# Low halves of the top-k's weights on VectorE, softmax 16 ticks earlier, two splits of v moved

## The chip, the cores and the metric

The kernel runs on one core of one Trainium2 chip. The metric is the device time of one execution in microseconds (us). The kernel before took 2052.27 us as the median of three runs (2051.45, 2052.27 and 2065.59). Engines are named as the profile names them: PE is TensorE's matmul part and PEld its weight load, DVE is VectorE, ACT is ScalarE, POOL is GpSimd, and SP is SyncE, which issues the weight transfers.

## The reference

The program computes a three-block network on 256 tokens of width 1024, in f32: a first block with attention, a recurrent unit and a memory attention, then a PEER expert layer, then two layers of four mixers and a feed-forward each. The change lies in the expert layer alone:

```
q = (h @ w_q), 8 heads x 2 halves x 128
sc = q . sub_keys                      # 8 x 2 x 128 scores a token
top_v, top_i = top_k(sc, 16)           # per half
cand = top_v[0] + top_v[1]             # all pairs of the two halves
best, pos = top_k(cand, 16); idx = the pair's expert number (of 16384)
gate = softmax(best)
act = gelu(u[idx] . h)
out = sum over heads and k of (gate * act) * v[idx]
```

The kernel does not gather rows of u and v. It multiplies with all 16384 rows, as 128 blocks of 128 experts, and zeroes what no token chose: a matrix of gates, built from one-hot rows, multiplies the acts.

## The kernel before, in words

**Weights.** All weights come as one stream of 128x128 blocks in f32. Eight blocks are a slot. SP loads two slots with one transfer (`raw`, two buffers). For each slot ACT writes the rounded high half `whi` (L93) and a second engine writes the low half `wlo` = raw - whi (L96); there are three buffers of each. The second engine is DVE, or POOL where `pool_share` says so: (1, 1) is set in the top-k after the projection of a head pair is traced, and (0, 1) after the top-k. Each weight block then costs three matmuls of 256 columns (L178 to L180: high by high, high by low, low by high), so a slot is 24 matmuls. The transfer for a `raw` buffer waits until both low halves of the pair that was in it have been written.

**Order.** The instructions of each engine stand in one fixed order, which a planner makes when the kernel is built. It plans with its own costs: of what is ready it takes the earliest traced first, and the splits of a slot have priority over the rest. At run time each engine works through its order strictly and waits where an operand is late. `issue_after(x)` puts an instruction behind x on x's engine.

**Ticks.** Side work is traced by generators (`add`, `tick`, `_step`), stepped each time two weight blocks have been used: a tick is two weight blocks, or six matmuls. The PE instructions of a step go behind the last matmul traced.

**The expert layer** (`peer`, L744) has these stages.

1. Top-k (`topk`, L954). Eight units (four head pairs by two token halves), 22 ticks apart (`TK_PACE`). A unit makes scores on PE (`sc`, L970) and then works on DVE alone: `top16` for four score rows, the candidate sums `cd` (L985), `top16` for two heads, index arithmetic (`tf` L977, `ij`, `ijf` L996 to L1005), two one-hot picks (`oh` L1008 and L1011, `sl` L1013). `TK_LAST` ticks after the last unit the softmax `gates` is traced (`ge` L1020, Exp on ACT at L1022, then L1023 to L1025 into `slg`); 6 ticks later `turn` transposes `sl1`, `sl2` and `slg` on PE (`ptk`, L248). Meanwhile PE runs the rest of the query projection and then blocks of u (`u_block`, L766: eight weight blocks, `pu`, then a gelu into `ha` or `hb` at L773). The number of u blocks done when the top-k ends is `early`.
2. First build (`build`, L792, with c0 = 0). 32 steps of eight tokens: DVE makes one-hots (`e` L810 and L812, `e1g` L815), PE multiplies them (`pgb`, L823), ACT copies (`gs` L827), DVE adds (L830) and multiplies the gates into the acts of the blocks 0 to 63 (L836), or only stores gates where an act does not exist yet (L841). Beside it run 64 further u blocks (`u_while`). The acts of the blocks `early` to 63 come in this stage and are kept apart.
3. The first of v. `weighted(b, g)` splits the gated act of block b into `ga`, a high half on ACT (L191) and a low half on DVE (L192). `collapse` (L868) multiplies the kept acts, four blocks at a time, with their gates. Three u blocks (`FILL`) are traced with the collapses.
4. The v loop. For b from 0 to 124: trace `weighted(b + 2)`, then eight weight blocks of v into `acc`; after each odd b one further u block until all 128 are done. The second build (`more`, c0 = 64) runs beside it, one step in 10 ticks. `weighted(64)` needs it complete, so what is left of it then is traced at once (`finish`, L877).

Of the kernel before, what the change touches and what calls it, by code (L numbers as in the profile page):

```python
# [7 lines left out]
F32 = mybir.dt.float32  # L8
# [5 lines left out]
ALU = mybir.AluOpType  # L14
# [14 lines left out]
N_HA = 96  # L29
HALF = 64  # L30
TK_PACE = 22
TK_LAST = 64
FILL = 3
T_OH = 8
PACE = {0: 7.5, HALF: 10}
# [22 lines left out]
class Stream:  # L58
# [3 lines left out]
    def __init__(self, K, pool, w):  # L62
        self.K, self.pool, self.w = K, pool, w
        self.order = []
        self.ticked = 0
        self.raw = None
        self.cur = None
        self.pool_share = (0, 1)

    def _dram(self, i):  # L70
        return self.w[i].rearrange("p (b c) -> p b c", c=P)
# [7 lines left out]
    def _slot(self):  # L79
        K, nc = self.K, self.K.nc  # L80
        n = len(self.order) // 8
        with K.tc.high_priority(offset=PRIO):
            if n % 2 == 0 and n:
                self.raw = self.pool.tile([P, 16, P], F32, tag="raw", name="raw", bufs=RAW_BUFS)
                m = min(16, N_BLOCKS - n * 8)
                step = 16 if n > 2 else 8
                for b in range(0, m, step):
                    e = min(b + step, m)
                    nc.sync.dma_start(out=self.raw[:, b:e, :], in_=self._dram(n // 2)[:, b:e, :])
            src = self.raw[:, (n % 2) * 8:(n % 2) * 8 + 8, :]  # L90
            hi = self.pool.tile([P, 8, P], F32R, tag="whi", name="whi", bufs=SLOT_BUFS)
            lo = self.pool.tile([P, 8, P], F32R, tag="wlo", name="wlo", bufs=SLOT_BUFS)
            self.on_scalar = nc.scalar.activation(out=hi, in_=src, func=AF.Copy).ins  # L93
            m, d = self.pool_share
            eng = nc.gpsimd if n * m % d < m and n else nc.vector
            i = eng.tensor_tensor(out=lo, in0=src, in1=hi.bitcast(F32), op=ALU.subtract)  # L96
            if eng is nc.vector:
                self.on_vector = i.ins
            else:
                self.on_pool = i.ins  # L100
        self.cur = (hi, lo)

    def blks(self, w, k, c, n=1):
# [25 lines left out]
def blocks(*tiles):  # L129
    return [t[:, i, :] for t in tiles for i in range(t.shape[1])]  # L130


class Core:
# [614 lines left out]
    def peer(self):  # L748
# [4 lines left out]
        tc, nc, a, ws = self.tc, self.nc, self.a, self.ws  # L753
        with ExitStack() as st:
# [6 lines left out]
            ga = [p.tile([P, 2, S], F32R, tag=f"ga{i}", name="ga") for i in range(2)]  # L761
# [3 lines left out]
            def h(b):  # L765
                return ha[:, b, :] if b < N_HA else hb[:, b - N_HA, :]  # L766
# [8 lines left out]
            def u_while(task, most, early):  # L775

                nonlocal ahead
                while task in self.tasks and ahead < most:
                    u_block(ahead, h(ahead + HALF if early <= ahead < HALF else ahead))
                    ahead += 1  # L780
                self.finish(task)
            ahead = 0
            with tc.tile_pool(name="tk", bufs=2) as tp:
                u_while(self.topk(tp, i1, i2, gt, iot), HALF, HALF)
            with tc.tile_pool(name="peg", bufs=1) as gp:
                hb = gp.tile([P, NBLK - N_HA, S], F32, tag="hb", name="hb")
                ga.append(gp.tile([P, 2, S], F32R, tag="ga2", name="ga"))
                ws.pool_share = (0, 1)
                n2, n1 = T_OH * P, T_OH * HALF
                e = self.tp.tile([P, 2, n2 + n1], F16, tag="ld", name="e", bufs=1)  # L790
                e2s = [e[:, i, 0:n2].rearrange("p (q c r) -> p q c r", c=P, r=2) for i in range(2)]
# [63 lines left out]

                early = ahead
                u_while(self.add(build(0, early), unit=1), HALF + early, early)
                assert ahead >= HALF

                def collapse(b0):  # L860

# [9 lines left out]
                def weighted(b, g):  # L871

                    if b == HALF:
                        self.finish(more)
                    src = h(b)
                    if b >= done:
                        with tc.issue_after(ws.on_vector):  # L877
                            nc.vector.tensor_tensor(out=src, in0=src, in1=h(b - done), op=ALU.mult)
                    self.split(g[:, 0, :], g[:, 1, :], src)
                    return g  # L880


                done = NBLK
                ready = [weighted(0, ga[0])]
                late = list(range(early, HALF, 4))
                for i in range(FILL):
                    for b in late[i * len(late) // FILL:(i + 1) * len(late) // FILL]:
# [11 lines left out]
                    self.mm3(acc[c // 2][:, c % 2, :], wh, wl, g[:, 0, :], g[:, 1, :],  # L899
                             first and c % 2 == 0, last and c % 2 == 1)  # L900

                ready.append(weighted(1, ga[1]))
                for b in range(NBLK - LAST):
                    if b + 2 < NBLK - LAST:
                        ready.append(weighted(b + 2, ga[(b + 2) % 3]))
# [9 lines left out]
            with tc.tile_pool(name="per", bufs=1) as gp:  # L915
# [6 lines left out]
                for c in range(KD):  # L922
                    for i, g in enumerate(tail):
                        v_cols(c, NBLK - LAST + i, g, False, i == LAST - 1)
                    if c % 2:
                        for d in (c - 1, c):
                            xc = self.x[:, d, :]
                            nc.vector.scalar_tensor_tensor(out=xc, in0=acc[d // 2][:, d % 2, :], scalar=1.0 / G_SCALE,
                                                           in1=xc, op0=ALU.mult, op1=ALU.add)
# [26 lines left out]
    def topk(self, tp, i1, i2, gt, iot):  # L956
        nc, a, ws = self.nc, self.a, self.ws
# [57 lines left out]
        def gates(t):  # L1015

            bv = bvs[t].rearrange("p (h k) -> p h k", k=16)
            e = tp.tile([P, 8, 16], F32, tag="ge", name="ge")
            sm = tp.tile([P, 2, 8], F32, tag="gs", name="gs")
            nc.vector.tensor_tensor(out=e, in0=bv, in1=bv[:, :, 0:1].to_broadcast([P, 8, 16]), op=ALU.subtract)  # L1020
            with self.tc.issue_after(ws.on_scalar):
                nc.scalar.activation(out=e, in_=e, func=AF.Exp)  # L1022
            nc.vector.tensor_reduce(out=sm[:, 0, :], in_=e, axis=AX.X, op=ALU.add)  # L1023
            nc.vector.reciprocal(out=sm[:, 1, :], in_=sm[:, 0, :])
            nc.vector.scalar_tensor_tensor(out=slg[t].rearrange("p (h k) -> p h k", k=16), in0=e, scalar=G_SCALE,  # L1025
                                           in1=sm[:, 1, :, None].to_broadcast([P, 8, 16]),
                                           op0=ALU.mult, op1=ALU.mult)

        def turn(t):

            ts = slice(t * P, t * P + P)
            pt = self.bg.tile([P, 3, P], F32, tag="bg", name="ptk")
            for i, sl in enumerate((sl1[t], sl2[t], slg[t])):
                self.transpose(pt[:, i, :], sl)
            nc.scalar.activation(out=i1[:, ts], in_=pt[:, 0, :], func=AF.Copy)
            nc.scalar.activation(out=i2[:, ts], in_=pt[:, 1, :], func=AF.Copy)
            nc.scalar.activation(out=gt[:, 0, ts], in_=pt[:, 2, :], func=AF.Copy)
            nc.vector.tensor_tensor(out=gt[:, 1, ts], in0=pt[:, 2, :], in1=gt[:, 0, ts], op=ALU.subtract)
            if t == 0:
                self.dump("sl1", sl1[0])  # L1040
                self.dump("sl2", sl2[0])
                self.dump("slg", slg[0])
# [3 lines left out]
        def picks():  # L1046
            with self.tc.issue_after(ws.on_vector):
                nc.gpsimd.tensor_copy(io, self.cst[:, None, C_IO:C_IO + 16].to_broadcast([P, 32, 16]))
            for hq in range(4):
                for t in range(2):  # L1050
                    while hq not in qts:
                        yield 1
                    unit(hq, t, qts[hq])
                    if hq == t == 1:
                        with self.tc.issue_after(ws.on_pool):
                            nc.gpsimd.tensor_copy(iot, self.cst[:, C_IO:C_IO + P, None].to_broadcast([P, P, 2]))
                    yield TK_PACE

            yield TK_LAST
            for t in range(2):  # L1060
                gates(t)
            yield 6
            for t in range(2):
                turn(t)
            yield 4

        task = self.add(picks(), unit=1)
        n = self.ld.shape[1] - 4
        for hq in range(1, 4):
            qt = tp.tile([P, 4, S], F32, tag="qt", name="qt")  # L1070
            c0 = 4 * hq + (n if hq == 1 else 0)

            def ev(c, ps):
                nc.scalar.activation(out=qt[:, c - 4 * hq:c - 4 * hq + 2, :], in_=ps, func=AF.Copy)
            self.proj_b(("w_peer_q", 0, 0), 4 * hq + 4, KD, self.hh, self.hl, ev, c0=c0,
                        lead=4 * hq + 4 - c0 if hq == 1 else 0)
            ws.pool_share = (1, 1)
            qts[hq] = Cat(blocks(self.ld[:, 4:4 + n, :], qt[:, n:, :])) if hq == 1 else qt
        return task

# [569 lines left out]
```

## Time and profile before

| what | value |
|---|---|
| median of three runs | 2052.27 us |
| the profiled execution's own time | 2051.29 us |
| its span, first to last instruction | 2049.5 us |
| PE busy, granted clock | 2006.7 us (98%), 0.993 of full |
| DVE busy | 1673.3 us (82%) |
| ACT busy | 1159.0 us (57%) |
| POOL busy | 277.9 us (14%), 146.2 us of it `wlo` |
| transfers | 364.73 MB read from memory, 179 GB/s over the span |

PE's busy share says how much of the span holds matmuls; what is left is idle time. A granted clock of 1.00 is 2.4 GHz, one of 0.50 is 1.2 GHz. POOL is busy with `wlo` from 311 us to 483 us, in the top-k. The top-k's last transposes stand at 485 us, the first product of the first build at 495 us, the first of v at 690 us and the end of the second build at 919 us.

### The profile page before, as it was taken

To read this page: it belongs to the slowest core of one execution; us is meant where nothing else is said; L and a number is where in the kernel's file an instruction comes from. 1 tells how busy PE (TensorE), PEld (TensorE's weight loads), DVE (VectorE), ACT (ScalarE), POOL (GpSimd) and SP (SyncE) were. 2 spreads that over 40 slices of the span, in tenths; PEclk is the share of its full clock that TensorE was granted. 3 is DMA by queue.
4 is the path that set the end of the run, shared out by engine and by line. 5 is a ranking of instruction groups with operands and counts; after the bars stand their busy time and mean duration, and the time that the engine had idled before them with its cause. 6 is when DMAs were issued, how large, how long until landed. Compare 5 with 4: busy or idle time off the path is not lost.

```text
span 2049.5 us, 41488 instructions
## 1 busy us (share of the span) xinstructions
PE 2006.7 (98%) x16818; PEld 1952.2 (95%) x16818; DVE 1673.3 (82%) x3281; ACT 1159.0 (57%) x1906; POOL 277.9 (14%) x173
## 2 busy tenths in 40 slices
PE   8999999999999999989999999999999999999999
PEld 7989999999999999989999889999999989999997
DVE  7877779999999999995568999978555999977554
ACT  6688654445555555544456565566445665466443
POOL 2212207883000000000000101200000101200000
PEclk9999999999999999999999999999999999999999
DMA  5345554454454455454554644555555644554554
GB/s 216 144 133 172 205 205 182 174 197 165 167 183 166 168 184 184 167 184 162 189 195 163 220 162 146 195 195 186 197 194 188 224 158 149 188 188 178 198 195 154
DMA packets 57019, 370.01 MB, mean 181 GB/s; under 512 B 6587, under 2 KB 10236, under 8 KB 13564
## 3 DMA queue, kind: packets, MB, share of 16 engines
q1 hardware_dynamic: 50256, 357.06, 48.4%
q10 hardware_dynamic: 6572, 10.31, 1.7%
q8 instruction: 131, 2.15, 0.4%
q14 instruction: 60, 0.49, 0.1%
HBM read 364.73 MB, written 2.62 MB: 179 GB/s over the span
## 4 chain that ended last, share of the span: by engine, by line
PE 68%; DVE 19%; issue 2%; ACT 2%; DMA 1%; ACTq 0%; DVEq 0%
PE acc L178 5%; PE acc L179 5%; PE acc L180 5%; PE mm L178 5%; PE mm L179 5%; PE mm L180 5%; PE pu L180 3%; PE pu L178 3%; PE pu L179 3%; PE pg L180 3%; PE pg L178 3%; PE pg L179 3%; DVE wlo L96 3%; PE pp L180 2%; PE pp L179 2%
## 5 line engine op out<-in xcount | busy, mean ns | idle before, releaser
L93 ACT ACTIVATE whi<-raw 128x1024 fp32r<-128x1024 f32 x677 | 717.5, 1061 | 738.7 <-DMA raw<-in_w 166.1
L96 DVE TENSOR_TENSOR wlo<-raw,whi 128x1024 fp32r<-128x1024 f32 x618 | 765.6, 1240 | 308.7 <-ACT whi L93 306.5
L180 PE MATMUL pu<-hh,wlo 128*128 128x256 f32 x1024 | 286.5, 280 | 2.1 <-POOL wlo L96 2.1
L178 PE MATMUL pu<-hh,whi 128*128 128x256 f32 x1024 | 285.2, 278 | 1.1 <-ACT whi L93 1.1
L180 PE MATMUL mm<-hh,wlo 128*128 128x256 f32 x1008 | 280.7, 279 | 5.1 <-DVE wlo L96 5.0
L179 PE MATMUL pu<-hl,whi 128*128 128x256 f32 x1024 | 283.8, 277 | 0.0
L178 PE MATMUL mm<-hh,whi 128*128 128x256 f32 x1008 | 281.0, 279 | 0.0
L179 PE MATMUL mm<-hl,whi 128*128 128x256 f32 x1008 | 280.4, 278 | 0.0
L178 PE MATMUL acc<-ga,whi 128*128 128x256 f32 x1000 | 277.4, 280 | 2.3 <-ACT ga L191 2.3
L179 PE MATMUL acc<-ga,whi 128*128 128x256 f32 x1000 | 277.5, 278 | 1.1 <-DVE ga L192 1.1
L180 PE MATMUL acc<-ga,wlo 128*128 128x256 f32 x1000 | 276.6, 278 | 0.0
L180 PEld LDWEIGHTS mm<-hh,wlo 128*128 128x128 f32 x1008 | 190.2, 189 | 8.1 <-DVE wlo L96 6.9
L178 PE MATMUL pg<-hh,whi 128*128 128x256 f32 x704 | 197.3, 280 | 0.0
L180 PE MATMUL pg<-hh,wlo 128*128 128x256 f32 x704 | 196.6, 279 | 0.5 <-DVE wlo L96 0.5
L179 PE MATMUL pg<-hl,whi 128*128 128x256 f32 x704 | 196.4, 279 | 0.0
L180 PEld LDWEIGHTS pu<-hh,wlo 128*128 128x128 f32 x1024 | 193.1, 189 | 2.3 <-POOL wlo L96 2.3
L178 PEld LDWEIGHTS pu<-hh,whi 128*128 128x128 f32 x1024 | 193.3, 189 | 1.7 <-ACT whi L93 1.5
L179 PEld LDWEIGHTS pu<-hl,whi 128*128 128x128 f32 x1024 | 193.1, 189 | 0.0
L178 PEld LDWEIGHTS mm<-hh,whi 128*128 128x128 f32 x1008 | 190.3, 189 | 1.4 <-issue 0.7
L179 PEld LDWEIGHTS acc<-ga,whi 128*128 128x128 f32 x1000 | 189.8, 190 | 1.3 <-DVE ga L192 1.3
L179 PEld LDWEIGHTS mm<-hl,whi 128*128 128x128 f32 x1008 | 190.0, 189 | 1.1 <-issue 0.8
L178 PEld LDWEIGHTS acc<-ga,whi 128*128 128x128 f32 x1000 | 188.1, 189 | 2.6 <-ACT ga L191 2.6
(413 smaller groups left out, 4901.3 us busy)
## 6 DMA issues: line engine op xcount, KB each, us to landing
raw<-in_w SPq DMA_DIRECT2D x336, 1024.0 KB
raw<-in_w SPq DMA_DIRECT2D x5, 512.0 KB
bias<-bias_scr ACTq DMA_DIRECT2D x4, 512.0 KB
bias_scr<-sbb ACTq DMA_DIRECT2D x16, 96.0 KB
cl<-in_cstl ACTq DMA_DIRECT2D x2, 576.0 KB
x<-in_xT SPq DMA_DIRECT2D x4, 256.0 KB
memt<-in_memT ACTq DMA_DIRECT2D x1, 1024.0 KB
keys<-in_keysT ACTq DMA_DIRECT2D x1, 1024.0 KB
```

What stands on the lines that cost most here:

```text
L93: self.on_scalar = nc.scalar.activation(out=hi, in_=src, func=AF.Copy).ins
L96: i = eng.tensor_tensor(out=lo, in0=src, in1=hi.bitcast(F32), op=ALU.subtract)
L178: mm(out, lhsT=wh, rhs=xh, start=start, stop=False)
L179: mm(out, lhsT=wh, rhs=xl, start=False, stop=False)
L180: self.on_pe = mm(out, lhsT=wl, rhs=xh, start=False, stop=stop).ins
```

## The change

All low halves of weights are made on DVE; `pool_share` is gone, and with it the 59 low halves on POOL. `TK_LAST` is 48 ticks in place of 64. In the third stage the splits for v's blocks 0 and 1 are both traced ahead of the collapses and of the three `FILL` blocks; before, that of block 1 was traced behind them. The index pattern `iot` (a POOL copy) names a DVE instruction in its `issue_after`, which orders nothing on POOL.

```diff
-TK_LAST = 64
+TK_LAST = 48
...
-        self.pool_share = (0, 1)
...
-            m, d = self.pool_share
-            eng = nc.gpsimd if n * m % d < m and n else nc.vector
-            i = eng.tensor_tensor(out=lo, in0=src, in1=hi.bitcast(F32), op=ALU.subtract)
-            if eng is nc.vector:
-                self.on_vector = i.ins
-            else:
-                self.on_pool = i.ins
+            i = nc.vector.tensor_tensor(out=lo, in0=src, in1=hi.bitcast(F32), op=ALU.subtract)
+            self.on_vector = i.ins
...
-                ws.pool_share = (0, 1)
...
-                assert ahead >= HALF
+                assert early >= 2 and ahead >= HALF
...
-                ready = [weighted(0, ga[0])]
+                ready = [weighted(b, ga[b]) for b in range(2)]
                 late = list(range(early, HALF, 4))
                 for i in range(FILL):
                     for b in late[i * len(late) // FILL:(i + 1) * len(late) // FILL]:
                         collapse(b)
                     u_block(ahead, h(ahead))
                     ahead += 1
...
-                ready.append(weighted(1, ga[1]))
                 for b in range(NBLK - LAST):
...
-                        with self.tc.issue_after(ws.on_pool):
+                        with self.tc.issue_after(ws.on_vector):
                             nc.gpsimd.tensor_copy(iot, ...)
...
-            ws.pool_share = (1, 1)
```

## Rows read from the trace of the kernel before

**Rows 1.** Windows, the top-k: stretch, us, then each engine's busy us, clock.

```profile
306.00:475.00 169.00, 169.00 (x1482) 168.83 (x1482) 167.25 (x506) 83.08 (x118) 139.85 (x58) 1.00 0.50 181
```

**Rows 2.** Source L970, the scores: count, ns min/median/max, first and last start.

```profile
L970 PE MATMUL sc<-keys,qt x48: 270/275/275, 335.8 to 416.4; 128*128 128x128 f32 x48
```

**Rows 3.** DVE by line, 306:485 us: busy us, mean ns of one, idle before.

```profile
L1008 DVE TENSOR_TENSOR oh<-ijf,io 128x512 f16<-128x512 f16 x16 | 25.1, 1569 | 0.0
L1011 DVE TENSOR_TENSOR oh<-oh,tf 128x512 f16<-128x512 f16 x16 | 23.8, 1485 | 0.3
L985 DVE TENSOR_TENSOR cd<-tv 128x96 f32<-128x96 f32 (+1 forms) x16 | 18.1, 1133 | 0.0
L1003 DVE SCALAR_TENSOR_TENSOR ijf<-ijf 128x32 f16<-128x32 f16 x8 | 14.7, 1838 | 0.0
...
L977 DVE CAST tf<-ti 128x64 f16<-128x64 uint32 x8 | 8.1, 1011 | 0.0
...
L1005 DVE TENSOR_TENSOR ijf<-bi,ijf 128x32 f16<-128x32 uint32 x8 | 8.0, 1001 | 0.0
...
L1001 DVE TENSOR_SCALAR ijf<-ijf 128x32 f16<-128x32 f16 x8 | 5.7, 714 | 0.3
```

**Rows 4.** DVE in order of time: start us, us; POOL idle, then busy.

```profile
469.37 0.27 DVE L985 TENSOR_TENSOR cd<-tv 128x128 f32<-128x128 f32 x1
...
474.84 0.68 DVE L1008 TENSOR_TENSOR oh<-ijf,io 128x512 f16<-128x512 f16 x1
...
475.44 0.18 DVE L1003 SCALAR_TENSOR_TENSOR ijf<-ijf 128x32 f16<-128x32 f16 x1
...
475.56 0.42 DVE L1011 TENSOR_TENSOR oh<-oh,tf 128x512 f16<-128x512 f16 x1
...
475.90 2.34 DVE L1005 TENSOR_TENSOR ijf<-bi,ijf 128x32 f16<-128x32 uint32 x1
```

**Rows 5.** POOL in order of time, its last three low halves.

```profile
475.68 7.82 POOL L96 TENSOR_TENSOR wlo<-raw,whi 128x1024 fp32r<-128x1024 f32 x3 [3.79 <-ACT whi L93]
```

**Rows 6.** POOL by line, whole span.

```profile
L96 POOL TENSOR_TENSOR wlo<-raw,whi 128x1024 fp32r<-128x1024 f32 x59 | 146.2, 2487 | 28.5 <-ACT whi L93 28.3
```

**Rows 7.** PE in order of time at the top-k's end; idle before, releaser.

```profile
478.24 0.38 PE L180 MATMUL pu<-hh,wlo 128*128 128x256 f32 x1 [2.08 <-POOL wlo L96]
...
485.34 0.33 PE L248 MATMUL ptk<-cst,slg 128*128 128x128 f32 x1 [1.13 <-DVE slg L1025]
```

**Rows 8.** Source L830, adds of the two builds, with their shapes.

```profile
L830 DVE TENSOR_TENSOR gs<-gs,pgb x128: 353/368/410, 498.7 to 919.9; 128x204 f32<-128x204 f32 x64, 128x216 f32<-128x216 f32 x64
```

**Rows 9.** DVE in order of time, before the first of v.

```profile
687.53 3.83 DVE L868 TENSOR_TENSOR ha<-ha,hb 128x1024 f32<-128x1024 f32 x4
691.27 1.22 DVE L96 TENSOR_TENSOR wlo<-raw,whi 128x1024 fp32r<-128x1024 f32 x1
692.40 1.09 DVE L192 TENSOR_TENSOR ga<-ha,ga 128x256 fp32r<-128x256 f32 x3
```

**Rows 10.** Windows: before the first of v; two stretches of low clock.

```profile
686.00:700.00 14.00, 12.22 (x91) 11.82 (x90) 11.42 (x17) 5.59 (x11) 0.00 (x0) 0.88 0.51 193
...
693.90:697.50 3.60, 3.60 (x20) 3.60 (x19) 2.29 (x3) 0.68 (x2) 0.00 (x0) 0.53 0.83 296
...
919.00:926.20 7.20, 4.89 (x25) 4.62 (x24) 3.04 (x11) 1.80 (x5) 0.00 (x0) 0.50 0.00 0
```

**Rows 11.** PE in order of time, end of the second build.

```profile
906.31 0.63 PE L823 MATMUL pgb<-e1g,e 128*128 128x128 f16 x8
...
911.28 0.63 PE L823 MATMUL pgb<-e1g,e 128*128 128x128 f16 x8
...
915.38 0.64 PE L823 MATMUL pgb<-e1g,e 128*128 128x128 f16 x8 [3.46 <-DVE e L810]
...
918.35 1.03 PE L823 MATMUL pgb<-e1g,e 128*128 128x128 f16 x8 [2.34 <-DVE e L810]
...
921.69 1.22 PE L178 MATMUL acc<-ga,whi 128*128 128x256 f32 x4 [2.31 <-ACT ga L191]
```

## Prediction

> **What bounds the kernel now.** The page's busy shares come first: PE holds matmuls for 2006.7 of 2049.5 us. The change adds no matmul and takes none away, so it can only move PE's idle time, some 43 us over the whole program, and the stretches in which PE had the lower clock. The windows by stage come next. In the top-k PE is busy without a gap while DVE is at 167.25 of 169 us and POOL at 139.85 [rows 1]: DVE is as full as PE, but nothing on PE waits for it there. What PE does lose near the change lies in three places, read from PE's order of time and its waits.
>
> *End of the top-k*: PE waits 2.08 us for a low half on POOL, then 1.13 us for `slg` [rows 7]. *Before the first of v*: 1.78 us idle of 14, then 3.6 us at about half clock [rows 10]. *End of the second build*: 3.46, 2.34 and 2.31 us, together 8.11 [rows 11], and from 919 us on the clock is at 0.50, which is 1.2 GHz; PE was busy 4.89 us there [rows 10], work of some 2.4 us at full clock, so 2.4 us lost. All three together are worth about 17 us, 0.8% of the time.
>
> **The change, part by part.** The sum is made against the profiled execution's 2051.29 us; the median of the runs is 0.98 us above that, which I add at the end.
>
> *59 low halves leave POOL.* A low half took 2.49 us there [rows 6] and takes 1.22 us on DVE, with a next instruction 1.13 us after its start [rows 9]. While POOL works, some DVE instructions of the top-k last about as long as a POOL one: `ijf` at L1005 took 2.34 us right after POOL began at 475.68 [rows 4, 5]; just before, with POOL idle, the one-hots took 0.68 and 0.42 and `ijf` 0.18, and `cd` 0.27 as POOL was only starting [rows 4]. Against these the means of the stretch [rows 3] give what the overlap costs: L1008 16 x (1.57 - 0.68) = 14.2, L1011 16 x (1.49 - 0.42) = 17.0, L985 16 x (1.13 - 0.27) = 13.8, L1003 8 x (1.84 - 0.18) = 13.3, and with the same 0.18 for L977, L1005 and L1001 6.6, 6.6 and 4.3: 75.8 us of DVE's time, which goes.
>
> The Trainium skill (Perfetto Trace Analysis, Optimizing Scalar/DVE Operations) advises, where DVE is saturated, to move work off it, to ScalarE or even GpSimd, though it adds that for GpSimd this may not help because the two share a port. By the advice alone the change goes the wrong way and the sum would be that of the last rival below; rows 3 to 5 bear out the caveat.
>
> *They come to DVE.* PE uses a slot (24 matmuls) in 24 x 169/1482 = 2.74 us [rows 1]. The top-k now ends 32 weight blocks sooner, that is 10.9 us, four slots, so 55 of the 59 lie in it: 55 x 1.13 = 62.2 us. DVE's work up to the softmax falls by 75.8 - 62.2 = 13.6 us. It stays full: over 306 to 475 us, 167.25 less 75.8 x 169/179 leaves 95.7, plus 62 slots x 1.13 = 70, 166 of 169.
>
> The new wait is that each low half now stands in DVE's strict order behind top-k work. Behind it are the matmuls of its slot and, through the release of `raw`, SP's next transfer. What hides it: POOL's 2.49 us hid completely in this stretch (PE full [rows 1]), so DVE may be at least 2.49 - 1.22 = 1.3 us late free of cost. No row shows DVE doing top-k and low halves together for long. From below: no wait at all. From above: units follow each other every (416.4 - 335.8 - 0.8)/5 = 16.0 us on PE [rows 2]; a unit has 95.7/8 = 12.0 us of DVE work, and 16.0 us hold 5.8 slots, 6.6 us; if the planner took a unit for short and put it all ahead, 2.6 us a unit, 21 us for eight. The second build is the nearest case, DVE full with low halves in its order and no wait in PE until its end. I take +2.
>
> *End of the top-k.* The low half that PE waited 2.08 us for comes 2.49 - 1.22 = 1.3 us sooner: -1.3. The Exps and what ACT does around them stay. The transposes: PE gets there 10.9 + 1.3 us sooner, at 472.0 in the old count, and `slg`, old 485.3, comes 13.6 sooner, at 471.7. That is even, with nothing to spare: I leave the old 1.13 as it is. Ends: -1.1, and +4 if all 59 low halves still come ahead.
>
> *Fewer u blocks in the top-k.* Sixteen ticks are 32 weight blocks, four u blocks. The first build adds 204 elements = 4 tokens x 51 blocks [rows 8], so `early` was 51 and becomes 47. The 64 blocks beside the first build and the three of `FILL` stay, so u blocks left for the v loop go from 10 (128 - 118; 216/4 = 54 = 118 - 64 [rows 8]) to 14. They move four blocks of PE work from the top-k to the v loop at no cost on PE. DVE multiplies four more late gates at the v loop's end, when the second build is long over: hidden; if DVE were still full there, four short multiplications of 256 elements.
>
> *Collapses.* Thirteen late blocks took 691.27 - 687.53 = 3.74 us on DVE, straight ahead of a low half and of the splits of `ga` [rows 9]. They become 17: +1.15 us. Block 0's split, traced ahead of the collapses already, still ran after all of them, in one row of three with its successors' [rows 9]; so I expect little from tracing block 1's early too. Its bounds: -3.5 (idle and low clock gone) to 0. I take 0, and +1.15 for the collapses, as PE waits for what they hold up. `iot` without its order has only constants to wait for, and nobody waits for it but SP's queue: 0.
>
> *End of the second build.* Its step k falls due at tick 11 + 10k of the v loop. `weighted(64)` forces the rest when 62 blocks of v and 10 of u are through, 72 x 4 = 288 ticks: steps 28 to 31 are forced, the four rows of products [rows 11]. With 14 blocks of u it is 304 ticks: step 29 is due at 301, so two are forced. From step 29 to block 64 of v DVE's chain took 921.69 - 911.28 = 10.4 us [rows 11]. PE now has 3 ticks, then blocks 62 and 63, 11 ticks x 0.685 = 7.5 us, and the products' own 1.9. That leaves 1 us of wait; as DVE must also make the low halves and splits of these blocks I take 3. So -5.1 of 8.11; the low clock I leave. Ends: 0 and -10.5.
>
> Sum: +2 - 1.3 + 1.15 - 5.1 = -3.2; 2051.29 - 3.2 + 0.98 = 2049.0 us.
>
> **The rivals.**
> 1. *DVE's order holds up PE* (slower). The price per unit is up to 2.6 us. It decides where waits in the top-k pass 5 us. For it: 98% load, no comparable row, and collapses that ran 3.7 us ahead of a low half that PE then waited for [rows 9]. Against it: splits have priority, and the second build. Halfway (10 us, 8 more than I took) it gives 2057, in full 2068; low clock behind each wait could add more. Chance 0.22.
> 2. *The second build's end keeps its wait*, DVE being full up to it whatever is forced: 2049.0 + 5.1 = 2054. The spacing of 4.1 and 3.0 us between forced steps speaks for DVE as the limit; 10.9 us more for the same steps speaks against. Chance 0.13.
> 3. *All of it goes well*: no waits in the top-k (-2), `slg` on time (-1.1), the first of v without a wait (-4.6), the build's end without wait or low clock (-5.4): 2036. Chance 0.11.
> 4. *The long DVE rows are not POOL's doing.* Then nothing is freed and 62 us come on top of a DVE with 2 us to spare: some 2051 + 60 = 2111. Rows 4 and 5 speak plainly against it. The advice of the Trainium skill's page named above would lead here. Chance 0.02.
>
> **How the numbers follow.** My own case has 0.52, with 2042 to 2054 as its range (build's end -10.5 to 0, top-k 0 to 5). The range reaches to 2060, over most of rival 1's halfway case and rival 2, and down to 2039, into rival 3; what is left out is about 0.15. Within 1% of 2052.27, about what a measurement of this kernel can tell from no change, is 2031.7 to 2072.8. All three idle places gone would be 17 us, not 20.5: faster 0.02. Slower needs rival 1 in full with low clock, or rival 4: 0.05. The rest, 0.93, is within.
>
> **What would show it.** POOL free of `wlo`; L1008, L1011, L1003, L985 near 0.68, 0.42, 0.18 and 0.27 us; adds of 188 and 200 elements in place of 204 and 216; two products in a row at the second build's end with under 4 us of idle PE; the transposes some 11 us sooner. PE waits on `wlo` of DVE above 5 us in the top-k would make the prediction wrong, and so would three waits still standing before block 64 of v.

## The result: a half per cent faster, and what the profile after shows

Over 20 runs each, the changed kernel took 2049.92 us in the median (2037.88 to 2056.41) and the kernel before 2059.74 us (2050.50 to 2073.20). The ratio is 0.9949 with a 95% interval of [0.993, 0.9967]: 10.5 us faster, between 6.8 and 14.4. The profiled execution took 2048.76 us, 2047.0 of it span, at a mean granted clock of 0.997.

The time forecast (2049.0 us) and its case (within 1%) hold. The size of the change does not: I had summed -3.2 us, and measured is three times that. The time still came out because the three runs shown of before were low ones: two of the three are the second and third lowest of its twenty, and their median is 7.5 us under the median of all.

The page after says PE 2010.7 us busy (98%), DVE 1656.2 (81%), POOL 132.0 (6%); POOL has no `wlo` any more. The lines of DVE in the top-k (busy us, mean ns of one, idle before) answer to [rows 3]:

```profile
L93 DVE TENSOR_TENSOR wlo<-raw,whi 128x1024 fp32r<-128x1024 f32 x57 | 69.1, 1214 | 6.3 <-ACT whi L92 3.5 <-PE pu L173 2.6
L1000 DVE TENSOR_TENSOR oh<-ijf,io 128x512 f16<-128x512 f16 x16 | 10.9, 682 | 0.0
...
L1003 DVE TENSOR_TENSOR oh<-oh,tf 128x512 f16<-128x512 f16 x16 | 6.7, 419 | 0.0
...
L977 DVE TENSOR_TENSOR cd<-tv 128x96 f32<-128x96 f32 (+1 forms) x16 | 4.1, 257 | 0.0
...
L969 DVE CAST tf<-ti 128x64 f16<-128x64 uint32 x8 | 1.5, 186 | 0.0
L997 DVE TENSOR_TENSOR ijf<-bi,ijf 128x32 f16<-128x32 uint32 x8 | 1.4, 181 | 0.0
...
L995 DVE SCALAR_TENSOR_TENSOR ijf<-ijf 128x32 f16<-128x32 f16 x8 | 1.4, 177 | 0.0
```

Each fell to the value that the few undisturbed rows of before had shown: 1569 to 682 ns, 1485 to 419, 1133 to 257, 1838 to 177. The windows (stretch, its length, then PE, PEld, DVE, ACT and POOL with counts, clock) say what that bought:

```profile
306.00:464.00 158.00, 157.96 (x1384) 157.85 (x1385) 151.68 (x567) 77.35 (x110) 1.00 (x1) 1.00 0.50 181
917.00:920.50 3.50, 3.50 (x18) 3.50 (x18) 0.17 (x1) 0.00 (x0) 0.00 (x0) 0.50 0.30 124
1000.00:1025.00 25.00, 25.00 (x215) 25.00 (x214) 13.60 (x18) 12.29 (x18) 0.00 (x0) 1.00 0.53 186
```

With all low halves on it DVE has 6 us of 158 to spare, where before it had under 2 of 169 [rows 1], and PE loses nothing there. The other two stretches come up below. PE in order of time, first at the top-k's end, answers to [rows 7]:

```profile
464.85 0.39 PE L172 MATMUL pu<-hh,whi 128*128 128x256 f32 x1 [0.37 <-ACT whi L92]
465.07 0.28 PE L173 MATMUL pu<-hl,whi 128*128 128x256 f32 x1
466.11 0.39 PE L174 MATMUL pu<-hh,wlo 128*128 128x256 f32 x1 [0.76 <-DVE wlo L93]
...
470.65 0.27 PE L242 MATMUL ptk<-cst,slg 128*128 128x128 f32 x1
```

The transposes wait for nothing. What is late instead is the slot behind the softmax. ACT and DVE, each in order of time, show why:

```profile
460.23 0.31 ACT L1014 ACTIVATE ge<-ge 128x128 f32<-128x128 f32 x1
460.56 1.28 ACT L767 ACT_TABLE_LOAD   x1
461.85 0.39 ACT L767 ACTIVATE ha<-pu 128x256 f32<-128x256 f32 x1
462.24 1.28 ACT L1014 ACT_TABLE_LOAD   x1
463.54 0.31 ACT L1014 ACTIVATE ge<-ge 128x128 f32<-128x128 f32 x1
463.76 1.04 ACT L92 ACTIVATE whi<-raw 128x1024 fp32r<-128x1024 f32 x1
```

```profile
463.88 0.29 DVE L1015 TENSOR_REDUCE gs<-ge 128x8 f32<-128x128 f32 x1 [3.02 <-ACT ge L1014]
...
464.83 1.23 DVE L93 TENSOR_TENSOR wlo<-raw,whi 128x1024 fp32r<-128x1024 f32 x1
```

A gelu between the two Exps makes ACT load its tables twice more; the high half stands behind all of it, and DVE, waiting 3.02 us for the second Exp, has the low half behind the rest of the softmax. ACT's order there was the same before the change, and PE waited for its high half then too, 0.47 us that my prediction left out:

```profile
475.66 0.39 PE L178 MATMUL pu<-hh,whi 128*128 128x256 f32 x1 [0.47 <-ACT whi L93]
```

Before the first of v, DVE's order answers to [rows 9], and PE's waits lie under it:

```profile
675.99 4.64 DVE L861 TENSOR_TENSOR ha<-ha,hb 128x1024 f32<-128x1024 f32 x4
680.53 1.23 DVE L93 TENSOR_TENSOR wlo<-raw,whi 128x1024 fp32r<-128x1024 f32 x1
681.67 0.43 DVE L861 TENSOR_TENSOR ha<-ha,hb 128x256 f32<-128x256 f32 x1
682.00 1.10 DVE L186 TENSOR_TENSOR ga<-ha,ga 128x256 fp32r<-128x256 f32 x3
```

```profile
680.31 0.39 PE L172 MATMUL pu<-hh,whi 128*128 128x256 f32 x1 [0.64 <-ACT whi L92]
...
682.49 0.39 PE L173 MATMUL acc<-ga,whi 128*128 128x256 f32 x1 [1.67 <-DVE ga L186]
```

The splits of both blocks, now traced ahead of all collapses, still run behind them: 2.31 us idle where it was 1.78. The end of the second build (PE in order of time) answers to [rows 11], and the source view of the adds to [rows 8]:

```profile
908.66 0.63 PE L816 MATMUL pgb<-e1g,e 128*128 128x128 f16 x8
...
911.90 0.63 PE L816 MATMUL pgb<-e1g,e 128*128 128x128 f16 x8 [0.49 <-DVE e L803]
916.10 1.22 PE L172 MATMUL acc<-ga,whi 128*128 128x256 f32 x4 [3.56 <-ACT ga L185]
```

```profile
L823 DVE TENSOR_TENSOR gs<-gs,pgb x128: 330/346/364, 484.7 to 914.3; 128x188 f32<-128x188 f32 x64, 128x200 f32<-128x200 f32 x64
```

188 and 200 elements, that is 47 and 50 blocks, two products in a row, and 4.05 us idle in place of 8.11. The clock of 0.50 behind it stayed.

**What blurs all this.** Between 1000 and 1025 us, well behind the change, both kernels' PE is busy all 25 us at full granted clock, and before, it did more in it:

```profile
1000.00:1025.00 25.00, 25.00 (x223) 25.00 (x223) 14.12 (x19) 12.69 (x19) 0.00 (x0) 1.00 0.51 190
```

223 matmuls against 215. PE starts one matmul of 256 columns after another in one of two steady distances, and after's rows in order of time show both:

```profile
461.82 0.28 PE L174 MATMUL pu<-hh,wlo 128*128 128x256 f32 x1
...
464.20 0.28 PE L174 MATMUL pu<-hh,wlo 128*128 128x256 f32 x1
...
1009.74 0.28 PE L172 MATMUL acc<-ga,whi 128*128 128x256 f32 x1
...
1011.16 0.28 PE L172 MATMUL acc<-ga,whi 128*128 128x256 f32 x1
```

21 matmuls in the first pair's 2.38 us, 113.3 ns each; 12 in the second's 1.42 us, 118 ns (117.9 over longer stretches). In this profile the wide distance holds from 920 to 1122 us, about 8 us lost for no reason that the kernels differ in. So I compare the stage (from the first `sc` to the last `acc` product) with this taken out: its length less 4.6 ns for every matmul in a stretch of the wide distance, counted from PE's rows. It went from 795.4 - 1.3 = 794.1 us to 795.9 - 10.4 = 785.5: the 8.6 us that the two lengths hide.

### The profile page after: what moved, and what is told of

The parts are those of the page before. It is cut to its first block, busy times and chain, and to the rows that moved or that the text cites. A ratio compares the mean times of both kernels' runs of the same rounds, so it can differ in the third digit from the quotient of the medians.

```text
span 2047.0 us, 41487 instructions
## 1 busy us (share of the span) xinstructions
PE 2010.7 (98%) x16818; PEld 1956.5 (96%) x16818; DVE 1656.2 (81%) x3345; ACT 1157.3 (57%) x1906; POOL 132.0 (6%) x114
## 4 chain that ended last, share of the span: by engine, by line
PE 71%; DVE 12%; DMA 3%; ACT 3%; issue 2%; POOL 0%; ACTq 0%; DVEq 0%; POOLq 0%
PE acc L172 6%; PE acc L173 6%; PE acc L174 6%; PE mm L173 5%; PE mm L172 5%; PE mm L174 5%; DVE wlo L93 4%; PE pu L174 3%; DMA raw<-in_w 3%; PE pu L172 3%; PE pg L174 3%; PE pu L173 3%; PE pg L172 3%; PE pg L173 3%; PE mml L173 2%; PE mml L174 2%
## 5 line engine op out<-in xcount | busy, mean ns | idle before, releaser
L93 DVE TENSOR_TENSOR wlo<-raw,whi 128x1024 fp32r<-128x1024 f32 x677 | 834.1, 1235 | 322.0 <-ACT whi L92 315.2
```

The lines of the kernel that those rows point to most:

```text
L93: i = nc.vector.tensor_tensor(out=lo, in0=src, in1=hi.bitcast(F32), op=ALU.subtract)
```

## The experiments

My theory: three local effects add up. DVE, freed of POOL's blocking, reaches the softmax in time; `TK_LAST` shortens the second build's end; the moved splits do nothing. Rivals: the parts work only together, or the gain is the matmuls' distance and no wait. The table holds one profile for each kernel. The "even" stage is the stage's length without the wide distance; the next three columns are PE's idle time at the top-k's end, before the first of v and at the second build's end; "low" is time lost at a granted clock of 0.50, at some 0.1 us a matmul; all in us.

| kernel | ratio to before, 95% | stage | even | top-k's end | before v | build's end | low |
|---|---|---|---|---|---|---|---|
| before | | 795.4 | 794.1 | 3.68 | 1.78 | 8.11 | 4.8 |
| before_again | | 801.6 | 793.5 | 0.72 | 2.08 | 8.53 | 2.0 |
| before_third | | 800.3 | 797.9 | 6.61 | 1.48 | 8.08 | 4.0 |
| split_only | 1.0007 [0.9987, 1.0028] | 801.8 | 795.3 | 4.10 | 1.81 | 7.90 | 5.0 |
| tk48_only | 1.0008 [0.9988, 1.0027] | 805.3 | 799.3 | 8.14 | 3.34 | 4.05 | 6.2 |
| dve_only | 0.9977 [0.9954, 1.0001] | 788.1 | 786.3 | 0 | 1.59 | 7.91 | 0.9 |
| after | 0.9949 [0.993, 0.9967] | 795.9 | 785.5 | 1.13 | 2.31 | 4.05 | 1.6 |
| after_again | 0.9924 [0.9896, 0.9952] | 787.5 | 786.1 | 0.92 | 2.89 | 4.06 | 3.2 |
| collapse_late | 0.9959 [0.9934, 0.9983] | 794.4 | 785.8 | 1.21 | 3.00 | 4.05 | 2.5 |
| tk40 | 0.9951 [0.9925, 0.9978] | 785.2 | 783.5 | 1.03 | 3.17 | 1.90 | 2.5 |
| splits_first | 0.9944 [0.9917, 0.9971] | 790.0 | 787.8 | 1.49 | 2.67 | 4.05 | 3.2 |
| pace9 | 0.9897 [0.9856, 0.9939] | 781.6 | 779.7 | 1.71 | 1.93 | 0 | 1.7 |
| pace9_splits_first | 0.9890 [0.9859, 0.9921] | 777.1 | 775.7 | 1.10 | 0.83 | 0 | 0 |
| pool_memset | | 797.2 | 789.2 | 1.66 | 3.19 | 4.05 | 4.3 |

**split_only**: before, with the splits moved and nothing else.

```diff
-                ready = [weighted(0, ga[0])]
+                ready = [weighted(b, ga[b]) for b in range(2)]
...
-                ready.append(weighted(1, ga[1]))
```

> The kernel before with both first splits of v traced ahead of the late acts' products, and nothing else. The planner's order comes out the same on every engine, so this is a second sample of the kernel before: ratio 1.000 within the interval. Theory A: its profile shows the same idle places and the same span within 1 us. Rival C: its profile has the same idle places but other stretches at 117.9 ns, and so another span by several us.

Ratio 1.0007, and the order of instructions on every engine is the one of before: the planner puts them in the same places. This part of the change does nothing, so split_only's profile is another of the kernel before.

**tk48_only**: before, with the softmax 16 ticks earlier.

```diff
-TK_LAST = 64
+TK_LAST = 48
```

> The kernel before with TK_LAST 48 alone, low halves still on GpSimd. Theory A: the transposes stand 10.9 us sooner on PE but slg comes no sooner, so PE waits 10 to 12 us there; early becomes 47, and the second build's end loses about 4 of its 8 us of idle. In all +5 to +8 us, ratio about 1.003. Rival B (it is POOL that costs): about 0, the early softmax being free or a gain. Rival C: idle as in A, time up to 7 us off the sum.

Ratio 1.0008. The build's end is halved as in after, and the top-k's end takes it back. PE in order of time, and ACT's row behind the first:

```profile
476.65 0.58 PE L178 MATMUL pu<-hh,whi 128*128 128x256 f32 x1 [5.95 <-ACT whi L93]
...
479.24 0.58 PE L180 MATMUL pu<-hh,wlo 128*128 128x256 f32 x1 [1.78 <-POOL wlo L96]
```

```profile
475.35 0.31 ACT L1022 ACTIVATE ge<-ge 128x128 f32<-128x128 f32 x1 [7.47 <-DVE ge L1020]
475.56 1.04 ACT L93 ACTIVATE whi<-raw 128x1024 fp32r<-128x1024 f32 x1
```

The Exp stands earlier in ACT's order, DVE is not there yet, and the next slot's high half waits behind the Exp. I had expected 10 to 12 us of wait there and a ratio of about 1.003; it is 8.14 us, and the interval ends below that. What I had as two independent terms hangs together: the earlier softmax needs the time that DVE gets back.

**dve_only**: after, with `TK_LAST` and the splits as before.

```diff
-TK_LAST = 48
+TK_LAST = 64
...
-                ready = [weighted(b, ga[b]) for b in range(2)]
+                ready = [weighted(0, ga[0])]
...
+                ready.append(weighted(1, ga[1]))
```

> The change without its softmax and split parts: low halves of the top-k on VectorE, TK_LAST 64. Theory A (sum of PE's idle places, as predicted): the low half before the softmax's end comes sooner (wait 2.1 to about 0.8 us), the transposes wait 0 instead of 1.1 us, the low clock after that place goes (1.5 us); early stays 51, so four steps of the second build are still forced and 8 us of idle stay there. In all -3 to -5 us, ratio about 0.998. Rival B (the gain is POOL off the shared path, and nothing else): the whole -10 us, ratio 0.995, already here. Rival C (spacing of matmuls, 113.3 or 117.9 ns, taken anew at each disturbance, decides most): idle as in A, but the time can lie 7 us off the sum either way, and the stretches at 117.9 ns account for it.

Ratio 0.9977, its interval reaching just to no change. PE has no wait at the top-k's end, and the build's end is that of before (PE in order of time):

```profile
911.45 1.04 PE L816 MATMUL pgb<-e1g,e 128*128 128x128 f16 x8 [3.43 <-DVE e L803]
914.66 1.03 PE L816 MATMUL pgb<-e1g,e 128*128 128x128 f16 x8 [2.17 <-DVE e L803]
918.00 1.22 PE L172 MATMUL acc<-ga,whi 128*128 128x256 f32 x4 [2.31 <-ACT ga L185]
```

That settles the two places: the first is the move to DVE, the second is `TK_LAST`. In the even stage dve_only is already where after is (786.3 against 785.5 to 786.1): what `TK_LAST` wins at the build's end, 3.9 us, it gives back at the softmax (0.9 to 1.2), before v (0.7 to 1.4) and in low clock (0.7 to 2.3). The runs are less even than the profiles. dve_only's profiled execution (2045.35 us) was the second fastest of its twelve, whose median is 2051.61; its ratio is worth 4.7 us, as theory A had it, and not the 9 us of its profile's stage. Its interval meets that of after's twenty runs. It does not meet that of after_again below, which was measured against the same runs of before. So `TK_LAST` may add some us to the move; how much, and where, the profiles don't show.

**after_again**: the changed kernel unaltered, beside these three.

> The changed kernel once more. Theory A: ratio 0.995 as measured before, profile with the same idle places as the first. Rival C: same idle places, but the stretches at 117.9 ns lie elsewhere than at 620 to 670 and 920 to 1100 us, and the span moves by their length times 4%.

Ratio 0.9924, and the gain is there again. Its profile is 4.57 us shorter in time than the first one (2044.19 against 2048.76); its stage is 8.4 us shorter, and the wide distance, which it does not have in the v loop, alone makes 9.0 of difference.

These runs show which part brings the gain. With the low halves on POOL, `TK_LAST` 48 changes nothing (tk48_only, 1.0008 [0.9988, 1.0027]). tk48_only and after differ in the low halves, in the splits, which did nothing in split_only, and in `iot`'s order, which no run tests alone; after is at 0.9949 [0.993, 0.9967]: at `TK_LAST` 48 it is the move to DVE that gains. At 64 the move alone is just not clear of no change.

**tk40**: `TK_LAST` = 40, so that the v loop has two more blocks of u to do before its 64th block.

```diff
-TK_LAST = 48
+TK_LAST = 40
```

> The changed kernel with TK_LAST 40 in place of 48: early 45, sixteen u blocks left for the v loop, so one step of the second build is forced in place of two. Theory A (forced steps set the wait at the second build's end; VectorE has slack at the softmax): idle there 4.1 to 1.5 us, the softmax's place unchanged at about 1 us: -2 to -4 us against the changed kernel, ratio 0.993. Rival B (VectorE's chain of the last steps sets it, however many are forced): idle there stays at 4 us; rival D: the Exps now wait for the last unit and hold up the high halves on ScalarE, as with TK_LAST 48 and the low halves on GpSimd (5.95 us): +3 to +6 us.

Ratio 0.9951, the same as after within the intervals. One row of products was forced, and at the build's end PE waited only for the splits:

```profile
912.62 0.73 PE L172 MATMUL acc<-ga,whi 128*128 128x256 f32 x4 [1.34 <-ACT ga L185]
913.91 0.38 PE L173 MATMUL acc<-ga,whi 128*128 128x256 f32 x1 [0.56 <-DVE ga L186]
```

The count of forced steps sets this wait: 8 us at four, 4 at two, 2 at one. The even stage is 2.3 us shorter, too little for the runs to tell.

**collapse_late**: four of the five collapses traced after the `FILL` blocks, meant to take them from in front of the splits.

```diff
                 for i in range(FILL):
-                    for b in late[i * len(late) // FILL:(i + 1) * len(late) // FILL]:
-                        collapse(b)
+                    if i == 0:
+                        collapse(late[0])
                     u_block(ahead, h(ahead))
                     ahead += 1
+                for b in late[1:]:
+                    collapse(b)
```

> The changed kernel with four of its five collapses traced behind the three u blocks (the first stays ahead, since those blocks take its slots). Theory A (the collapses on VectorE hold up a low half and the first splits): PE's idle before the first of v goes from 2.3 to 2.9 us to under 1 us, and the low clock after it, where there is one, goes: -1.5 to -4 us against the changed kernel. Rival: that wait is ScalarE's (it does the three high halves of the splits ahead of the weights'), so it stays at 2 us or more.

It misses its aim: DVE's order there came out as in after, all collapses still ahead of the splits, and the waits with it. It tells nothing of their cause, only how little the order of tracing does here.

**splits_first**: after, with the collapses made to follow block 1's low half on DVE.

```diff
-                            with tc.issue_after(ws.on_vector):
+                            with tc.issue_after(self.last_lo):
...
-                    self.split(g[:, 0, :], g[:, 1, :], src)
+                    self.last_lo = self.split(g[:, 0, :], g[:, 1, :], src)[1].ins
```

> The changed kernel with the collapses put behind the low half of block 1's split on VectorE (issue_after on that instruction in place of the last weight's low half), so that the two first splits and a weight's low half do run ahead of the late acts' products. Theory A (the collapses hold up what PE waits for before the first of v): idle there 2.3 to 2.9 us goes under 1 us, and any low clock after it goes: -1.5 to -3.5 us against the changed kernel, ratio to before about 0.991. Rival: ScalarE's high halves set that wait, or the collapses now hold up the next low half: 2 us or more stay.

Ratio 0.9944, no different from after. DVE in order of time:

```profile
681.78 0.42 DVE L186 TENSOR_TENSOR ga<-ha,ga 128x256 fp32r<-128x256 f32 x1
682.12 4.96 DVE L861 TENSOR_TENSOR ha<-ha,hb 128x1024 f32<-128x1024 f32 x5
...
687.33 3.49 DVE L93 TENSOR_TENSOR wlo<-raw,whi 128x1024 fp32r<-128x1024 f32 x3
```

and PE:

```profile
688.61 0.38 PE L174 MATMUL acc<-ga,wlo 128*128 128x256 f32 x1 [2.67 <-DVE wlo L93]
```

The splits do come first now, and PE no longer waits for them; it waits for the low halves that stand behind the 4.96 us of collapses. Theory A fails, and the second half of its rival is right: the collapses in one row hold up whatever stands behind them. They alone do not set the wait's size, as pace9_splits_first below shows.

**pace9**: the second build one step in 9 ticks in place of 10.

```diff
-PACE = {0: 7.5, HALF: 10}
+PACE = {0: 7.5, HALF: 9}
```

> The changed kernel with a step of the second build every 9 ticks in place of 10: step 31 is due at tick 290 of 304, none is forced. If the forced steps are the cause of the wait at the build's end: idle there 4.1 to under 1 us, -3 to -5 us against the changed kernel. If VectorE's work is the bound (98% load at a step in 10 ticks): the wait comes back spread over the v loop as waits for one-hots, low halves or splits, 4 us or more in all: 0 to +6 us.

Ratio 0.9897 [0.9856, 0.9939]: no step is forced and the wait at the build's end and its low clock are gone. The even stage falls by some 6 us against after. The intervals of pace9 and after meet at their ends (0.993 to 0.9939), so the step from one to the other rests on this and on the next run together.

**pace9_splits_first**: both edits.

> Both mends: a step of the second build every 9 ticks, and the collapses behind the two first splits. Theory A: the two add; idle between the first scores and the last product of v about 4 us (1.8 at the start, 1 to 2 at the softmax, under 1 before v, 0 at the build's end), ratio to before 0.987 to 0.989. If steps every 9 ticks need the idle before v to let VectorE catch up, a wait comes up in the v loop, 1 to 4 us.

2033.90 us, ratio 0.9890 [0.9859, 0.9921], its interval below that of after's twenty runs (though not below that of after_again): the best version run. The windows of its v loop up to 1080 us:

```profile
690.00:1080.00 390.00, 390.00 (x3539) 388.89 (x3538) 316.31 (x647) 207.11 (x339) 0.21 (x1) 1.00 0.53 187
```

PE has no idle time and no low clock, and from 674 to 1085 us its only wait is this line of the waits (sum, times, longest):

```profile
PE acc L174 <- DVE wlo L93: 0.8, 1, 0.8
```

That wait is 0.83 us where splits_first has 2.67, with the same row of collapses (DVE in order of time):

```profile
677.19 4.96 DVE L861 TENSOR_TENSOR ha<-ha,hb 128x1024 f32<-128x1024 f32 x5
```

Up to this place the two kernels have the same order on every engine; they part only at 692 us. So the pace is not what made this wait shorter: DVE began the row 5.65 us before PE ran dry in this execution, 3.82 us in splits_first, where PE had also waited for one-hots at 655 and 668 us. The size of the wait before v differs by some 2 us between executions of the same order, and one profile of each kernel can't tell smaller effects there.

**pool_memset**: after, with eight memsets of 128x256 on POOL beside each low half of the top-k, to see whether a busy POOL as such slows DVE or brings the wide distance.

```diff
+            if self.dummy is not None:
+                for _ in range(8):
+                    nc.gpsimd.memset(self.dummy, 0.0)
```

> The changed kernel, and beside each slot of weights in the top-k eight memsets of 128x256 on GpSimd into a tile that nobody reads: GpSimd busy there without making anything that PE or VectorE waits for. Theory C with GpSimd as its cause (its activity keeps the matmuls of the top-k at 117.9 ns, as in three of four profiles with low halves on it and none of six without): 117.9 ns from 321 to about 470 us, span 6 us longer. If the spacing has to do with who hands PE its weights, or is chance: back to 113.3 ns at about 350 us, as in the changed kernel.

2053.82 us in one run. POOL was busy 115.57 of the 158 us from 306 to 464 us, and DVE's lines with two inputs did not move:

```profile
L94 DVE TENSOR_TENSOR wlo<-raw,whi 128x1024 fp32r<-128x1024 f32 x58 | 70.2, 1212 | 6.8 <-ACT whi L93 6.8
L1005 DVE TENSOR_TENSOR oh<-ijf,io 128x512 f16<-128x512 f16 x16 | 10.9, 679 | 0.0
...
L1008 DVE TENSOR_TENSOR oh<-oh,tf 128x512 f16<-128x512 f16 x16 | 6.6, 416 | 0.0
```

A POOL instruction that reads two operands lengthened the one-hot to 1569 ns; one that only writes leaves it at 679. The Trainium skill (SBUF — State Buffer, Who interferes with whom) says so: a DVE instruction with two SBUF inputs contends with a GpSimd instruction that reads SBUF, not with one that only writes. Both kernels agree with it. Lines with one input, of which that sentence does not speak, moved a little beside the memsets (the cast into `tf` from 186 to 223 ns) and much beside POOL's low halves (1011 ns, L977 in [rows 3]). Beside the memsets the top-k's matmuls stood at the narrow distance, as in after.

**before_again** and **before_third**: the kernel before, one profile each, to see what its first one had of its own.

> The kernel before, one more profile. Its idle places and low clock should repeat (idle 15 us and 12 us of low clock between the first scores and the last product of v), and the rest of that stage, without them and without the stretches at 117.9 ns, should be 767 us again. Theory C (spacing drawn anew at disturbances): the top-k from 321 to about 480 us is at 117.9 ns in some profiles of it and not in others.

> The kernel before, another profile, for the count of profiles of it whose top-k runs at 117.9 ns (three of four so far with low halves on GpSimd). If GpSimd's low halves bring it about, most likely once more 117.9 ns from 321 to about 480 us; idle and low clock as before, rest of the stage 767 to 768 us.

2059.94 and 2056.84 us. PE's idle time in the stage was 16.3 and 18.7 us, where the first profile had 15.2; at the top-k's end alone it was 0.72 and 6.61 us. Windows of 25 us in the middle of the top-k separate two kinds of profile; split_only (the kernel before in effect) first, then before_third:

```profile
400.00:425.00 25.00, 25.00 (x216) 25.00 (x215) 24.76 (x75) 10.94 (x18) 19.68 (x9) 1.00 0.50 184
```

```profile
400.00:425.00 25.00, 25.00 (x223) 25.00 (x223) 24.73 (x65) 11.82 (x18) 21.28 (x10) 1.00 0.56 204
```

Three of the five profiles with low halves on POOL (split_only, tk48_only, before_again) have the wide distance there, from 309 to 321 us on until between 470 and 500, some 6 us; the first of before, which I argued from, and before_third do not. Nor do any of the nine with the low halves on DVE, pool_memset among them. Chance alone would sort three such profiles all among those five in 10 of 364 draws, so this is a hint and not shown. Three of those nine (after, collapse_late, pool_memset) have it from about 920 to 1100 us instead, some 8 us each.

## Why the prediction was right, step by step, and where its sizes were off

Means over the four profiles of before (split_only among them) and three of after (collapse_late among them, whose order is the same) put the even stage at 795.2 and 785.8 us: -9.4, against my -3.2.

- **POOL's blocking** (75.8 us of DVE time freed): right. The freed time from the rows after is 16 x (0.887 + 1.066 + 0.876) for the one-hots and `cd`, 8 x 1.661 for L1003 of before, and the three small ones: 76 us. Two lines that I had not listed fell as well, L996 of before from 279 to 170 ns and L999 from 458 to 180, another 4 us. The step after it, DVE 166 of 169 loaded, was a little too full; 151.68 of 158 is 96%.
- **Waits on low halves in the top-k, +2**: failed, in the good direction; up to the softmax there are none. At 96% load the planner's order, which puts the splits first, cost PE nothing, so rival 1 falls, its halfway case too.
- **End of the top-k, -1.3**: too small. Idle time fell from a mean of 3.78 us to 1.09. I left the 1.13 us for `slg` standing, missed the 0.47 us for `whi`, and did not count the low clock behind the 2.08 us wait (479 to 482 us in the profile I had), which none of these three profiles after has there, nor dve_only (pace9, splits_first and pool_memset have some).
- **Collapses, +1.15, and the moved splits, 0**: right. The collapses took 4.64 + 0.43 = 5.07 us where they took 3.74, and the wait before v rose from a mean of 1.79 to 2.73.
- **Second build's end, -5.1**: right in its mechanism (four forced steps to two) and 1 us too large, 8.16 to 4.05. The low clock stayed, as I left it. Rival 2 falls.
- **What the sum did not have**: low clock in all places together 3.95 to 2.43 us, and some 2 us more. Half a us of these are waits of PE for one-hots in the first build (a mean of 1.08 before, 0.56 after, and from 0 to 3.35 in single profiles); the rest I can't assign to a place.

Sum of the means: -2.7 + 0.9 - 4.1 - 1.5 - 2.0 = -9.4. Rival 3 had the top-k right and the other two places wrong. Rival 4 falls by the DVE lines: the advice that the prediction quotes from the Trainium skill (Perfetto Trace Analysis, Optimizing Scalar/DVE Operations), to take work off a full DVE, would have been wrong here (tk48_only 1.0008, after 0.9949), the caveat that goes with it right. Whether the wide distance adds to the measured 10.5 us (some 6 us in the top-k of some runs before, 8 in the v loop of some after) the profiles can't say.

The largest single error was none of these terms: it was to set the base at 2052.27. A spread from 2051.45 to 2065.59 in three runs, with nothing in one profile to explain it, said that the base was open by some 7 us, twice my sum. That the forecast came within 1 us of the median is luck: a base 7.5 us too low and a gain 7.3 us too small cancelled.

## What to carry to other kernels

When two engines block each other, read the price from the same instruction with the other engine idle and then busy; here it was worth moving the work back even to an engine 99% loaded, which was 96% loaded afterwards. A step that is moved earlier on one engine needs its producer on another to be earlier too: the earlier softmax alone gained nothing. Look for what produces the wait in a row and spread that: reordering what stood behind the collapses moved the wait to the next in line (spreading the collapses was not tried), while starting the second build's steps one tick closer took 4 us of wait and its low clock away.

## What the runs showed of the hardware that I had not expected

PE at full granted clock, without a gap, runs its 256-column matmuls 113.3 or 117.9 ns apart, for tens to some 200 us at a time, and the profile's busy time and clock are the same for both; only the count of matmuls in a window tells them apart (223 or 215 in 25 us). In the profiles the distance changes mostly at disturbances, a wait of PE or the `sc` matmuls. The Trainium skill (TensorE: Matmul & The Clock Gate, Wait — 56ns, not 53.3ns?) gives the distance of back-to-back matmuls as their columns at 2.4 GHz plus about 2.5 ns, by which 256 columns would be an estimated 109 ns; here each matmul has a weight load beside it, and both measured values are above that. What sets the distance was not found.
